# Attention projections as seven block products: four of the six projections of each layer in two pairs, pooling inputs and gates between them, pooled tiles and gates through DRAM

## The chip, the core and the metric

The kernel runs on one core of one Trainium2 chip. A core has five engines that run side by side, each taking its own instructions strictly in the order in which they were queued: TensorE (PE in the profile; PEld is its loading of weights), VectorE (DVE), ScalarE (ACT), GpSimd (POOL) and SyncE (SP), which here issues nearly all transfers between DRAM and the on-chip memories. The metric is the device time of one execution in microseconds, lower is better.

## The reference, cut to what matters

Two layers run over 512 tokens of 1024 channels. Each layer is a half-step feed-forward block, a mixer, and another half-step feed-forward block. The change is in the mixer:

```python
proj = h @ w_in                      # h: 512 x 1024
qa, ka, va, ub, qc, kc, vc, f_lin, g_lin = split(proj)   # six of 512 columns, ub 512, f 8, g 3 x 1024
ya = chunked_attention(qa, ka, va, rel_bias)     # 8 heads of 64
yb = pool_w(trailing_means(ub) - ub)             # 4 groups, windows 2, 4, 8, 16
yc = forgetting_attention(qc, kc, vc, f_lin)     # 8 heads of 64
merged = sum_n sigmoid(g_n) * (y_n @ w_branch_n) # n = a, b, c
x += gate2 * (merged @ w_out)
```

So the mixer multiplies the same `h` with weights for six attention projections, four pooling inputs of 128 channels, and 24 gate tiles of 128 channels. The result must agree with 32-bit floats.

## The kernel before, in words

Activations are kept transposed, as channels (partitions) by tokens. The kernel multiplies in a rounded 32-bit format: each operand is split into a rounded part `hi` and a remainder `lo`, and one 32-bit product is three matmuls, hi*hi, hi*lo and lo*hi (`triple`, L119 to L121). The normalised `h` lies split in `hhi` and `hlo`, as eight blocks of 128 channels. A weight chunk (`wchunk`, L266 to L279) is a transfer of 512 KB into a `raw` buffer (two of them), a cast on ACT to `whi` and a subtraction on DVE to `wlo` (three buffers each). A large pool of 17 buffers of 4 KB a partition, tag `b`, holds nearly everything else.

The code is Python that emits instructions in program order. A planner then orders each engine's queue by its own simulated times: an instruction that would wait can be overtaken by a later one whose operands are ready, and among ready ones the earlier in the program goes first. The programmer steers it by the order in the program, by `later(delay, fn)`, which emits `fn` when the counter `pe[0]` of issued matmuls (in units of one matmul of 512 columns) has advanced by `delay`, and by explicit orderings (`issue_after`). `behind(...)` in `wchunk` puts a chunk's cast and subtraction behind the newest piece of the norm.

The mixer (`Mixer.run`) goes in this order. (1) `norm.back` finishes `h` in two token halves, eight pieces each, with one ACT and two DVE instructions a piece (L371 to L374). (2) Three projections one after the other, `proj_qk` for qa and ka and `proj_v` for va, each four chunks of weights and 32 triples of 512 columns, with tokens as the stationary side; the first one starts on the first token half while the second is being normalised. The eight log-forget columns (`forget`) lie between them. Queries and keys get a norm per head (a square on ACT, a sum on DVE at L808, a Newton iteration of small DVE instructions at L293 to L295, a scaling at L826), and are then transposed on PE and split (`turn`, L831 to L846). (3) `attention` for branch a: 32 tiles of logits, and between them a generator of filler matmuls, nine units for each tile. Its filler is the projections qc, kc and vc. (4) `attention` for branch c; its filler is the gates and the merge of branch a. (5) After that the four pooling inputs (`pool_front`: 24 matmuls, then sums over shifted columns on POOL at L1033, then DVE), the gates and merge of c, and the gates and merge of b (`merge_units`; a gate is 24 matmuls and a tanh, a merge step 12 matmuls). (6) The output projection.

Beside this run the 144 modulation products, called dots here (`mod_step`, L206): each a 512 KB transfer and one DVE instruction over 1024 elements. `side_work` emits them in credit units as weight chunks are asked for: at rate `MOD_RATE` in the feed-forward blocks, and one a chunk in the merges of c and b. `mod_need` emits at once all that are still missing where they are needed.

The feed-forward blocks already use block products: two gate or up tiles and `h` are cut in two each way, and `seven` computes their product with seven block products in place of eight, from sums and differences of blocks of the weights (S1 to S4) and of `h` (T1 to T4, made by `Blocks` at L452 to L477 and kept split in eight `b` buffers).

## Time and profile before

| | us |
|---|---|
| median of 3 runs (lowest, highest) | 2408.19 (2405.26, 2410.62) |
| the profiled execution | 2409.17 |
| its span from the first to the last instruction | 2407.4 |
| PE busy (matmuls) | 2361.9 (98%) |
| PE loading weights | 2086.8 (87%) |
| DVE busy | 1728.9 (72%) |
| ACT busy | 1197.8 (50%) |
| POOL busy | 351.7 (15%) |
| HBM read, written | 312.16 MB, 6.38 MB |

The granted TensorE clock was 0.999 over the span. In this execution the first layer's mixer begins its projections at about 372 us and reaches the output projection at about 775 us; the second layer's is about 1190 us later. Matmuls are pipelined, so a matmul's recorded time is longer than the distance to the next one; the distance from start to start is what it costs when others follow. The table of stretches gives for each stretch its length, then for each engine the busy time and, in brackets, the number of instructions, then the granted clock, the busy share of the transfer engines and GB/s. The timeline gives start, duration, engine, line, operation, output and inputs, and in square brackets how long the engine had been idle before and what ended that. The list of waits gives total, count and longest.

### The profile page before, as it was taken

Reading aid. Unit: us, or ns where it says so; the run is one execution under the profiler, and the core shown is the slowest. Engines: PE = TensorE matmul, PEld = TensorE weight load, DVE = VectorE, ACT = ScalarE, POOL = GpSimd, SP = SyncE. Lnnn points to the kernel's source line nnn. Section 1 sums busy time; section 2 is a strip of 40 time slices with the busy share of each in tenths; the row PEclk is TensorE's granted clock in tenths of the full one; section 3 lists DMA queues with packets and bytes.
Section 4 is the critical chain, followed back from the end, with each engine's and each line's share of the span. In section 5 each row is a group of like instructions: output and inputs, shape, how many; then the busy total and the mean of one; then the engine's idle time right before and its main releaser. Section 6 shows DMA issues by size and latency. Waiting matters only on the chain. (4 is left out here: it accounts for less than half of the span.)

```text
span 2407.4 us, 36815 instructions
## 1 busy us (share of the span) xinstructions
PE 2361.9 (98%) x14106; PEld 2086.8 (87%) x14106; DVE 1728.9 (72%) x3070; ACT 1197.8 (50%) x2090; POOL 351.7 (15%) x423
## 2 busy tenths in 40 slices
PE   7999999999999999999999999999999999999999
PEld 5898988778878898989998989888788788989898
DVE  8987886787665476878577868777866755658583
ACT  5353545786632353535543636466765324536352
POOL 3000011144432210000100000112444322000000
PEclk9999999999999999999999999999999999999999
DMA  7534362323345524343325343623233554223322
GB/s 274 201 106 175 106 219 88 93 79 107 109 171 200 175 99 156 108 165 105 132 87 185 105 165 104 215 83 102 74 120 104 198 182 168 71 97 106 101 95 103
DMA packets 116436, 320.93 MB, mean 133 GB/s; under 512 B 11138, under 2 KB 13314, under 8 KB 116260
## 3 DMA queue, kind: packets, MB, share of 16 engines
q1 hardware_dynamic: 115106, 314.38, 38.8%
q0 software_dynamic: 1152, 4.19, 0.5%
q8 instruction: 111, 1.82, 0.3%
q14 instruction: 65, 0.53, 0.1%
q10 hardware_dynamic: 2, 0.00, 0.0%
HBM read 312.16 MB, written 6.38 MB: 132 GB/s over the span
## 5 line engine op out<-in xcount | busy, mean ns | idle before, releaser
L277 ACT CAST whi<-raw 128x1024 fp32r<-128x1024 f32 (+1 forms) x267 | 277.5, 1043 | 449.6 <-PE acc L120 251.7
L279 DVE TENSOR_TENSOR wlo<-raw,whi 128x1024 fp32r<-128x1024 f32 x259 | 321.1, 1242 | 168.2 <-ACT whi L277 165.0
L119 PE MATMUL acc<-b,whi 128*128 128x512 f32 (+1 forms) x960 | 361.8, 377 | 3.8 <-ACT whi L277 3.8
L121 PE MATMUL acc<-b,wlo 128*128 128x512 f32 (+1 forms) x960 | 358.0, 373 | 0.6 <-DVE wlo L279 0.6
L120 PE MATMUL acc<-b,whi 128*128 128x512 f32 (+1 forms) x960 | 358.5, 373 | 0.0
L119 PEld LDWEIGHTS acc<-b,whi 128*128 128x128 f32 x960 | 181.4, 189 | 36.0 <-ACT whi L277 4.6
L121 PEld LDWEIGHTS acc<-b,wlo 128*128 128x128 f32 x960 | 181.7, 189 | 33.1 <-DVE wlo L279 1.5
L120 PEld LDWEIGHTS acc<-b,whi 128*128 128x128 f32 x960 | 181.8, 189 | 30.1
L119 PE MATMUL acc<-hhi,whi 128*128 128x512 f32 x480 | 191.3, 400 | 7.2 <-DVE b L1051 3.1
L120 PE MATMUL acc<-hlo,whi 128*128 128x512 f32 x480 | 188.0, 392 | 1.1 <-DVE hlo L711 1.1
L121 PE MATMUL acc<-hhi,wlo 128*128 128x512 f32 x480 | 187.7, 392 | 0.3 <-DVE wlo L279 0.3
L385 DVE TENSOR_TENSOR ptb<-v,ptb 128x1024 fp32r<-128x1024 f32 x128 | 156.5, 1223 | 36.4 <-ACT ptb L384 36.2
L384 ACT CAST ptb<-v 128x1024 fp32r<-128x1024 f32 x128 | 134.1, 1050 | 92.8 <-DVE v L452 47.9
L384 ACT CAST whi<-raw 128x1024 fp32r<-128x1024 f32 (+1 forms) x128 | 106.7, 833 | 99.3 <-PE acc L120 56.2
L119 PE MATMUL acc<-whi,hhi 128*128 128x512 f32 x336 | 137.8, 411 | 0.9 <-DVE xv L385 0.9
L206 DVE CUSTOM_DVE_ANT_0 v<-v,b,badac 128x1024 f32<-128x1024 f32 x96 | 127.2, 1333 | 12.3 <-DMA v<-in_w_ada_dram 12.0
L121 PE MATMUL acc<-whi,hlo 128*128 128x512 f32 x336 | 131.9, 393 | 0.0
L120 PE MATMUL acc<-wlo,hhi 128*128 128x512 f32 x336 | 131.7, 392 | 0.0
L385 DVE TENSOR_TENSOR wlo<-raw,whi 128x1024 fp32r<-128x1024 f32 (+1 forms) x128 | 121.7, 950 | 6.4 <-ACT whi L384 4.6
L434 DVE SCALAR_TENSOR_TENSOR xv<-acc,modc,xv 128x512 f32<-128x512 f32 (+1 forms) x112 | 77.2, 690 | 64.1 <-PE acc L121 64.1
L119 PEld LDWEIGHTS acc<-hhi,whi 128*128 128x128 f32 x480 | 90.7, 189 | 26.1 <-DVE b L1051 4.0
L329 POOL TENSOR_TENSOR ssum<-ssum,t 128x256 f32<-128x256 f32 (+1 forms) x45 | 46.9, 1043 | 442.4 <-ACT t L328 442.2
(315 smaller groups left out, 6664.5 us busy)
## 6 DMA issues: line engine op xcount, KB each, us to landing
v<-in_w_ada_dram SPq DMA_DIRECT2D x96, 512.0 KB, 5.0
raw<-in_w_down_dram SPq DMA_DIRECT2D x88, 512.0 KB, 3.7
raw<-in_w_up_dram SPq DMA_DIRECT2D x82, 512.0 KB, 3.6
raw<-in_w_gate_dram SPq DMA_DIRECT2D x79, 512.0 KB, 3.6
raw<-in_w_ubg_dram SPq DMA_DIRECT2D x56, 512.0 KB, 3.5
b<-in_w_ada_dram SPq DMA_DIRECT2D x48, 512.0 KB, 4.7
raw<-in_w_qkv_dram SPq DMA_DIRECT2D x42, 512.0 KB, 3.8
raw<-in_w_branch_dram SPq DMA_DIRECT2D x24, 512.0 KB, 3.7
```

The source lines that it names most:

```text
L119: mm(o, lh, rh, start=start, stop=False)
L120: mm(o, lh, rl, start=False, stop=False)
L121: mm(o, ll, rh, start=False, stop=stop)
L206: dot = nc.vector.tensor_tensor_reduce(out=raw, in0=raw, in1=silc[0], scale=1.0, scalar=badac[:, l, j, d:d + 1], op0=ALU.mult, op1=ALU.add ...
L277: nc.scalar.copy(hi, raw)
L279: lo_eng.tensor_tensor(lo, raw, hi.bitcast(F32), op=ALU.subtract)
L329: nc.gpsimd.tensor_tensor(self.ssum[:, cols], self.ssum[:, cols], q, op=ALU.add)
L384: nc.scalar.copy(hi, src)
L385: nc.vector.tensor_tensor(lo, src, hi.bitcast(F32), op=ALU.subtract)
L434: nc.vector.scalar_tensor_tensor(x, acc_j, gate, x, op0=ALU.mult, op1=ALU.add)
```

## The change

The projections va and vc (columns 2 and 5 of the weights), and then qa and ka (columns 0 and 1), are computed as two pairs by a new function `wide`. Its `split_chunk` is the cast and subtraction of `wchunk`. A pair is a product of a 512 x 1024 `h` with 1024 x 1024 weights, cut in two each way. Seven block products P1 to P7 make it; each is 24 matmuls of 512 columns, so a pair is 168 in place of 192. The weights' sums and differences are made on DVE for each half product from unsplit chunks, and then split. The blocks T1 to T4 of `h` come from `Blocks`, now used in the mixer too; its steps are reordered so that T1 and T3 come first. Partial results are copied from PSUM to SBUF by ACT, the others added to them by DVE; `Values` and `Keys` then split the sums for attention. vc thus moves from the filler of attention a to the front. qc and kc stay there as before.

Between the block products stand other matmuls: all four pooling inputs behind P2 of the first pair, the first four gates of branch a (one after P6 of the first pair, one after P5 of the second, two at the end), and `forget`. The pooled tiles are made some 60 units later, with their shifted sums on DVE where they were on POOL, and go through DRAM until the merge. The gates of branch a are kept in DRAM too and read back as pairs; gates 4 to 7 of a fill attention a in vc's place, the gates of c fill attention c beside the merge of a, and the gates of b are made behind attention c. The dots of the merges start in the second half of attention c. In the feed-forward blocks the dots' rate in the down products goes from 1.0 to 1.9, 1.2, 1.6 and 1.2.

```diff
+    th_dram = [dr.tile([3, 4, P, 2 * T], F32, name=f"th_dram{l}") for l in range(L)]
+    u_dram = [dr.tile([4, P, 2, T], F32, name=f"u_dram{l}") for l in range(L)]
...
-            steps = ((self.h, 0), (self.h, 2), (self.t1_t3, 0), (self.split, 0), (self.t2_t4, 0), (self.split, 2))
-            self.todo = [lambda fn=fn, i=i + m: fn(i) for m in range(2) for fn, i in steps]
+            one = ((self.h, 0), (self.h, 2), (self.t1_t3, 0), (self.split, 0))
+            two = ((self.t2_t4, 0), (self.split, 2))
+            self.todo = [lambda fn=fn, i=i + m: fn(i) for steps in (one, two) for m in range(2) for fn, i in steps]
...
-                MOD_RATE[0] = 1.0
+                MOD_RATE[0] = (1.9, 1.2, 1.6, 1.2)[2 * l + s]
...
+    class Values:
...
+        def done(self, t):
+            b = st([P, H, 2, HD], F32R, self.tag, 4)
+            a3 = self.sums[:, t, :].rearrange("p (h d) -> p h d", h=H)
             for odd in range(2):
+                split_to(b[:, odd::2, odd, :], b[:, odd::2, 1 - odd, :], a3[:, odd::2, :])
...
+    class Keys:
...
+        def done(self, t, a=None):
+            a = self.sums[:, t, :] if a is None else a
             sq = t2(T)
             nc.scalar.activation(sq, a, AF.Square)
+            nc.vector.tensor_reduce(self.ss[:, t, :], sq.rearrange("p (h d) -> p h d", h=H), axis=AX.X, op=ALU.add)
...
+    def qkv_raw(l, col, kh, c, tag):
+        side_work()
+        raw = st([P, 2, T], F32, tag, {"b": NB, "raw": NRAW}[tag])
+        r0 = (4 * kh + 2 * c) * P
+        src = w_qkv[l, r0:r0 + 2 * P, col * T:(col + 1) * T].rearrange("(k p) c -> p k c", p=P)
+        last["dma"] = nc.sync.dma_start(raw, src).ins
+        return raw
+    def wide(l, cols, outs, blocks, order, pre=None):
+        first, second = outs
+        banks = {}
+        kept = {"a21": [], "s1": []}
+        two = (0, 1)
+        def bank(name):
+            if name not in banks:
+                banks[name] = [(mmt if name == "y" else acc)() for _ in two]
+            return banks[name]
+        def product(name, left, right, start):
+            o = bank(name)
+            for c in two:
+                hi, lo = left(c)
+                pairs = [(t, kk) for t in two for kk in two]
+                for n, (t, kk) in enumerate(pairs + pairs):
+                    bh, bl = blocks.operand(right)[2 * c + kk]
+                    tk = slice(t * P, (t + 1) * P)
+                    poll()
+                    if n < 4:
+                        mm(o[t], bh[:, tk], hi[:, kk, :], start=start and c == 0 and kk == 0, stop=False,
+                           skip_group_check=True)
+                        mm(o[t], bl[:, tk], hi[:, kk, :], start=False, stop=False, skip_group_check=True)
+                        pe[0] += 2.0
+                    else:
+                        mm(o[t], bh[:, tk], lo[:, kk, :], start=False, stop=c == 1 and kk == 1,
+                           skip_group_check=True)
+                        pe[0] += 1.0
+        def copy_out(name, out, t0, done=False):
+            for t in two:
+                nc.scalar.copy(out.sum_tile()[:, t0 + t, :], banks[name][t])
+                if done:
+                    out.done(t0 + t)
+        def add_out(name, out, t0):
+            for t in two:
+                s = out.sum_tile()[:, t0 + t, :]
+                nc.vector.tensor_tensor(s, banks[name][t], s, op=ALU.add)
+                out.done(t0 + t)
+        def p1():
+            if pre is None:
+                kept["a11"] = [qkv_raw(l, cols[0], 0, c, "b") for c in two]
+                product("x", lambda c: split_chunk(kept["a11"][c]), "B11", True)
+            else:
+                kept["a11"] = [p[2] for p in pre[:2]]
+                product("x", lambda c: pre[c][:2], "B11", True)
+            copy_out("x", first, 0)
+        def p2():
+            def left(c):
+                if pre is not None:
+                    return kept["a12"][c]
+                raw = qkv_raw(l, cols[0], 1, c, "raw")
+                parts = split_chunk(raw)
+                if "s2" in kept:
+                    minus(kept["s2"][c], raw, kept["s2"][c])
+                    kept["s4"] = kept["s2"]
+                return parts
+            product("y", left, "B21", True)
+            add_out("y", first, 0)
+        def left5(c):
+                if "ready" in kept and c == 0:
+                    return kept["ready"]
+                a21 = qkv_raw(l, cols[1], 0, c, "b")
+                a22 = qkv_raw(l, cols[1], 1, c, "raw")
+                s1 = st([P, 2, T], F32, "b", NB)
+                nc.vector.tensor_tensor(s1, a21, a22, op=ALU.add)
+                kept["a21"].append(a21)
+                kept["s1"].append(s1)
+                return split_chunk(s1)
+        def prep5():
+            kept["ready"] = left5(0)
+        def p5():
+            product("w", left5, "T1", True)
+            copy_out("w", second, 2)
+        def p6():
+            kept["s2"] = kept["s1"]
+            def left(c):
+                minus(kept["s2"][c], kept["s1"][c], kept["a11"][c])
+                return split_chunk(kept["s2"][c])
+            product("x", left, "T2", False)
+            copy_out("x", first, 2)
+        def p7():
+            def left(c):
+                minus(kept["a11"][c], kept["a11"][c], kept["a21"][c])
+                return split_chunk(kept["a11"][c])
+            product("x", left, "T3", False)
+            add_out("x", second, 2)
+        def p3():
+            def left(c):
+                if "s4" in kept:
+                    return split_chunk(kept["s4"][c])
+                raw = qkv_raw(l, cols[0], 1, c, "raw")
+                minus(kept["s2"][c], raw, kept["s2"][c])
+                return split_chunk(kept["s2"][c])
+            product("w", left, "B22", False)
+            add_out("w", first, 2)
+        def p4():
+            product("x", lambda c: split_chunk(qkv_raw(l, cols[1], 1, c, "raw")), "T4", False)
+            copy_out("x", second, 0, True)
+        steps = {"P1": p1, "P2": p2, "P3": p3, "P4": p4, "P5": p5, "P6": p6, "P7": p7}
+        if pre is not None:
+            kept["a12"] = [pre[2][:2], split_chunk(qkv_raw(l, cols[0], 1, 1, "raw"))]
+        for step in order:
+            if callable(step):
+                step(prep5)
+            else:
+                steps[step]()
+        first.begin()
+        second.begin()
...
+    def inputs(l, i, bank, w=None):
+        hi, lo = w or wchunk(w_ubg[l, i], (KD, P))
+        o = bank()
         for k in range(KD):
-            triple(pu, hi[:, k, :], lo[:, k, :], hhi[:, k, :], hlo[:, k, :], k == 0, k == KD - 1)
+            triple(o, hi[:, k, :], lo[:, k, :], hhi[:, k, :], hlo[:, k, :], k == 0, k == KD - 1)
+            yield
+        return o
+    def pool_in(l, g, bank, w=None):
+        pu = yield from inputs(l, g, bank, w)
         u = st([P, T + 16], F32, "b", NB)
         nc.gpsimd.memset(u[:, :16], 0.0)
         nc.scalar.copy(u[:, 16:], pu)
+        later(60 + 16 * g, lambda: pool_front(l, g, u))
+    def gate_in(l, n, d, bank, dest=None):
+        pg = yield from inputs(l, 4 + n * KD + d, bank)
+        th = t1(T) if dest is None else dest
+        nc.scalar.activation(th, pg, AF.Tanh, scale=0.5)
+        if dest is None:
+            nc.sync.dma_start(th_dram[l][n, d // 2, :, (d % 2) * T:(d % 2 + 1) * T], th)
+    def gate_pair(l, n, q, tag):
+        g = blk(tag, F32)
+        nc.sync.dma_start(g, th_dram[l][n, q].rearrange("p (a t) -> p a t", a=2))
+        return g
...
-            nc.gpsimd.tensor_tensor(nx[:, 16:], cur[:, 16:], cur[:, 16 - step:T + 16 - step], op=ALU.add)
+            nc.vector.tensor_tensor(nx[:, 16:], cur[:, 16:], cur[:, 16 - step:T + 16 - step], op=ALU.add)
...
-        b = st([P, 2, T], F32R, "ptb", 2)
+        b = blk("b")
         split_to(b[:, 0, :], b[:, 1, :], df)
-        return b
+        nc.sync.dma_start(u_dram[l][g], b.bitcast(F32))
...
-            self.pre = [qkv_chunk(self.l, 0, c, spare=t) for c, t in enumerate(("ptb", "ptb", "b"))]
+            self.pre = [qkv_chunk(self.l, 2, c, spare=t, keep=True) for c, t in enumerate(("ptb", "ptb", "b"))]
...
-            drain(proj_qk(l, 0, g8[:, 0:1], True, qa, self.pre, self.norm),
-                  proj_qk(l, 1, g[:, 1:2], False, ka), forget(l),
-                  proj_v(l, 2, "xv", va))
+            blocks = Blocks(self.norm.xa, modc[:, l, 3])
+            first_in = []
+            def ahead(_):
+                first_in.append(wchunk(w_ubg[l, 0], (KD, P)))
+            def second_half(prep):
+                self.norm.back(1, mmt)
+                blocks.schedule(4, 4)
+                drain(pool_in(l, 0, mmt, first_in[0]), pool_in(l, 1, mmt), pool_in(l, 2, mmt))
+                prep()
+                drain(pool_in(l, 3, mmt))
+                blocks.finish()
+            ga = [lambda _, d=d: drain(gate_in(l, 0, d, mmt)) for d in range(4)]
+            self.norm.back(0, mmt)
+            later(FRONT2, lambda: self.norm.front(1, mmt))
+            later(BACK2, lambda: self.norm.back(1, mmt))
+            wide(l, (2, 5), (Values("xv", va), Values("v2", vc)), blocks,
+                 (ahead, "P1", "P2", second_half, "P5", "P6", ga[0], "P3", "P7", lambda _: drain(forget(l)), "P4"), self.pre)
+            wide(l, (0, 1), (Keys(g8[:, 0:1], True, qa), Keys(g[:, 1:2], False, ka)), blocks,
+                 ("P1", "P5", ga[1], "P6", "P2", "P7", "P3", "P4"))
+            ga[2](None)
+            ga[3](None)
             finish_turns()
             turns.clear()
             heads[0] = 0
 
             def fill_a():
-                yield from proj_qk(l, 3, g8[:, 2:3], True, qc)
-                yield from proj_qk(l, 4, g[:, 3:4], False, kc)
-                yield from proj_v(l, 5, "v2", vc)
+                yield from proj_qk(l, 3, Keys(g8[:, 2:3], True, qc))
+                yield from proj_qk(l, 4, Keys(g[:, 3:4], False, kc))
+                for d in range(4, KD):
+                    yield from gate_in(l, 0, d, acc)
...
+            def gates_a(d):
+                yield
+                return m[d // 2][:, d % 2, :]
...
+            gb, gc = [], []
             def fill_c():
-                yield from merge_units(l, 0, ya, put_a)
-
-            attention(qc, kc, vc, lambda h: strip_c(l, h), yc, fill_c(), FILL_C, "c")
+                m.extend(gate_pair(l, 0, q, "xv") for q in range(4))
+                for d in range(3):
+                    yield from gate_in(l, 2, d, acc)
+                yield from merge_units(l, 0, ya, put_a, gates_a)
+                for d in range(3, KD):
+                    yield from gate_in(l, 2, d, acc)
+            pooled = []
+            def start_dots():
+                silc[0] = st([P, D], F32, "b", NB)
+                nc.sync.dma_start(silc[0], sil_dram.broadcast_to([P, D]))
+                in_ffn[0], mod_tag[0], MOD_RATE[0] = True, "b", 1.0
+            attention(qc, kc, vc, lambda h: strip_c(l, h), yc, fill_c(), FILL_C, "c",
+                      {4: start_dots})
             finish_turns()
             turns.clear()
+            wp = wpool_load(l)
+            for gi in range(4):
+                pooled.append(blk("b"))
+                nc.sync.dma_start(pooled[gi].bitcast(F32), u_dram[l][gi])
+            for d in range(4):
+                if d % 2 == 0:
+                    gb.append(blk("b", F32))
+                drain(gate_in(l, 1, d, acc, gb[d // 2][:, d % 2, :]))
             poll(True)
-            silc[0] = st([P, D], F32, "b", NB)
-            nc.sync.dma_start(silc[0], sil_dram.broadcast_to([P, D]))
-            wp = wpool_load(l)
-            mc = merge_units(l, 2, yc, put_c)
+            mc = merge_units(l, 2, yc, put_c, gates_c)
             for gi in range(4):
-                b = pool_front(l, gi)
-                later(60, lambda gi=gi, b=b: pool_back(l, gi, b, wp, yb))
-            in_ffn[0], mod_tag[0], MOD_RATE[0] = True, "b", 1.0
+                later(2 + 10 * gi, lambda gi=gi: pool_back(l, gi, pooled[gi], wp, yb))
             drain(mc)
             poll(True)
-            mb = merge_units(l, 1, yb, put_b)
+            mb = merge_units(l, 1, yb, put_b, gates_b)
             drain(mb)
```

248 lines of the change are left out of this document (119 added, 129 removed).

## The prediction

> **What bounds the kernel now.** First the page's busy times, then the stretches of the first layer's mixer, then single rows.
>
> ```profile
> PE   2361.9 (98%) x14106; PEld 2086.8 (87%) x14106; DVE 1728.9 (72%) x3070; ACT 1197.8 (50%) x2090; POOL 351.7 (15%) x423
> 160.00:170.00 10.00, 10.00 (x87) 10.00 (x86) 9.47 (x16) 6.33 (x11) 0.00 (x0) 1.00 0.34 105
> 300.00:345.00 45.00, 43.26 (x303) 40.06 (x302) 39.47 (x70) 19.88 (x32) 0.00 (x0) 0.98 0.61 207
> 372.00:394.00 22.00, 22.00 (x122) 18.65 (x121) 18.66 (x63) 11.62 (x27) 7.92 (x14) 1.00 0.13 50
> 394.00:447.00 53.00, 52.13 (x242) 41.39 (x242) 38.38 (x68) 35.14 (x50) 0.14 (x1) 1.00 0.31 96
> 447.00:545.00 98.00, 93.54 (x496) 76.49 (x495) 76.23 (x199) 74.85 (x164) 35.15 (x48) 1.00 0.29 87
> 545.00:640.00 95.00, 93.81 (x514) 79.16 (x513) 64.80 (x176) 60.36 (x150) 45.25 (x67) 1.00 0.35 115
> ```
>
> TensorE is busy for 98% of the span, and in the mixer's front (372 to 447 us: the three projections and forget) for 74.1 of 75 us. So matmuls are the time, and whoever removes one gains its place in the queue, if the other engines keep up. DVE is the one to watch: 57 of those 75 us, 76 of 98 in attention a, 65 of 95 in attention c. The first row is a feed-forward stretch with block products already in use: DVE 95% busy and PE not idle at all. A DVE that is nearly full does not by itself stop PE.
>
> What one matmul costs, from two rows of the second projection, 53 matmuls of 512 columns apart:
>
> ```profile
> 401.79 0.39 PE L119 MATMUL acc<-whi,hhi 128*128 128x512 f32 x1
> ...
> 413.80 0.39 PE L121 MATMUL acc<-whi,hlo 128*128 128x512 f32 x1
> ```
>
> 12.01 us by 53 is 0.227 us from start to start. That is my unit; 0.39 is only its length in the pipeline. The same holds on DVE:
>
> ```profile
> 159.44 0.68 DVE L385 TENSOR_TENSOR wlo<-raw,whi 128x512 fp32r<-128x512 f32 x1
> 160.04 0.68 DVE L452 TENSOR_TENSOR v<-raw,raw 128x512 f32<-128x512 f32 x1
> ...
> 163.65 0.42 DVE L515 TENSOR_TENSOR v<-v 128x256 f32<-128x256 f32 x1
> 163.99 0.42 DVE L515 TENSOR_TENSOR v<-mm,v 128x256 f32<-128x256 f32 x1
> ...
> 165.40 1.22 DVE L385 TENSOR_TENSOR ptb<-v,ptb 128x1024 fp32r<-128x1024 f32 x1
> 166.53 0.69 DVE L385 TENSOR_TENSOR b<-t,b 128x512 fp32r<-128x512 f32 x1
> ```
>
> Behind one another, a DVE instruction of 256, 512 or 1024 columns takes 0.34, 0.60 or 1.13 us from start to start, against 0.42, 0.68 and 1.22 recorded. Which of the two counts decides this case.
>
> **PE: what is removed.** A pair takes 7 x 24 = 168 matmuls in place of 192. Two pairs in two layers: 96 matmuls by 0.227 = 21.8 us less. All else on PE (pooling inputs, gates, merges, qc, kc) only changes place, matmul for matmul. Moved to the front, per layer: vc, four pooling inputs, four gates.
>
> **DVE: what is added.** Per layer 12 more weight splits (25 half products against 13 chunks of weights still to split in the front and vc), 16 sums and differences of weights, the blocks T (8 of 512, 4 of 1024), 12 additions of partial results, and 10 shifted sums from POOL: some 60 us, onto a DVE that had room for it over the layer, but mostly in the first pair. So I set DVE against PE there, from the end of P2 to the last split that P4 needs.
>
> PE: four pooling inputs, P5, P6, a gate, P3, P7, forget and half of P4, that is 244 units by 0.227 = 55.4 us, and 0.9 us that the row 394 to 447 shows idle already: 56.3.
>
> DVE, all of it earlier in the program than that last split:
>
> ```profile
> 386.87 1.08 DVE L371 TENSOR_TENSOR v<-mm,v 128x256 f32<-128x256 f32 x3 [0.79 <-PE mm L365]
> 387.89 0.50 PE L119 MATMUL acc<-ptb,hhi 128*128 128x512 f32 x1
> 393.60 2.36 DVE L279 TENSOR_TENSOR wlo<-raw,whi 128x1024 fp32r<-128x1024 f32 x2 [0.45 <-ACT whi L277]
> 441.15 1.21 DVE L902 TENSOR_TENSOR_SCAN t<-t 8x512 f32<-8x512 f32 x1
> ```
>
> - the rest of the second token half's norm: PE began that half at 387.89 us and DVE was through with it by about 393: 5 us
> - 1024 columns: splits of three pooling chunks, a gate, P4's two halves, T's four; in P5, P6, P3 and P7 two splits and two sums each: 26 by 1.13 = 29.4
> - 512 columns: T 8, additions after P2, P3 and P7 6, pooling 1+2+3+4 shifted sums and two more a tile: 32 by 0.60 = 19.2
> - 256 columns: two splits for each of six value tiles: 12 by 0.34 = 4.1
> - eight small pooling instructions, 1.2; forget's ten, of which the scan's 1.21 is the longest, 5 (estimate)
>
> Together 63.9 us against 56.3: PE waits 7.6 us a layer. From below: the pooled tiles (12 us of these 63.9) aren't needed until the merge; if they slipped into the second pair there would be no wait. From above: with recorded durations the list is 31.7 + 22.1 + 5.0 + 1.4 + 5.4 + 5.5 = 71.1, a wait of 14.8. I take 7.6, since the starts show the shorter steps, and the planner takes what is earlier in the program first.
>
> [...] The rows above, 0.60 us apart at 0.68 us recorded, speak for the shorter step.
>
> **The second pair.** DVE: 17 splits and 8 sums of 1024 (28.3), 6 additions, 8 sums of squares and 8 scalings of 512 (13.2), the last value tiles 1.4, 24 small Newton steps 4.8: 47.7 us against 240 units = 54.5 of PE. It keeps up. Its end is new: keys are complete only with P4, and before attention a lies nothing but two gates, 48 units = 10.9 us, where before it was all of va (96 units).
>
> ```profile
> 429.66 0.18 DVE L816 TENSOR_SCALAR nt_v<-qss 128x32 f32<-128x32 f32 x1
> ...
> 436.11 1.89 DVE L826 TENSOR_TENSOR ptb<-ptb,nt_z 128x512 f32<-128x512 f32 x3
> 448.40 1.40 ACT L840 ACTIVATE b<-mm,qkgc 64x512 fp32r<-64x512 f32 x2
> ```
>
> Behind P4: copies and squares on ACT some 2.4 us, a sum 0.6, small steps of both 4.8 (one alone took 429.66 to 436.11 with other work between), scalings 4.8, two gate splits 2.3: 14.9 us, 4.0 too much. Then all four turns of the queries stand ahead of the first key's: 16 ACT instructions by 0.70, 11 us, in which PE has only the filler qc, if its casts came first. So between nothing and 15 us; three chunks' buffers hold 16 us of filler, and the old transposes waited too. I take 2.5 a layer.
>
> **ACT, transfers, queues.** ACT had 46.8 of 75 us in the front; 16 more casts, the copies and the T blocks fill a longer stage to some 75%: nothing, as long as DVE is the later one. Added traffic is 3 MB of weights and 12 MB of gates and pooled tiles a layer, in stretches with a transfer share of 0.13 to 0.35: nothing. All go by SP's queue; a gate's write waits there for its tanh, and weight loads behind it with it. A load lands in 3.8 us, and a half product lasts 12 units = 2.7, with two `raw` buffers ahead; P6, P7 and most of P1 and P3 don't need them. If that cover were gone, each such write would cost up to 3 us.
>
> **What goes away.**
>
> ```profile
> PE acc L119 <- ACT whi L277: 6.2, 4, 2.3
> PE acc L119 <- DVE b L1051: 3.1, 2, 1.6
> 560.64 1.05 ACT L277 CAST whi<-raw 128x1024 fp32r<-128x1024 f32 x1
> 561.74 0.50 PE L119 MATMUL acc<-hhi,whi 128*128 128x512 f32 x1 [1.19 <-ACT whi L277]
> 689.77 2.05 DVE L206 CUSTOM_DVE_ANT_0 b<-b,b,badac 128x1024 f32<-128x1024 f32 x1
> ```
>
> PE's wait for pooled outputs, 3.1 us in both layers. The wait at 560 us behind vc's value splits, 1.4 in each layer with the matmul's ramp, 2.8. At 300 to 345 us the first feed-forward block emitted its ten missing dots at once (`mod_need` wants 32, the credits had given 22); at rate 1.9 they give 34, so the longest of those four waits, 2.3, goes. Added: in attention c some six dots a layer, 1.3 to 2.05 us each, on a DVE busy 65 of 95 us; I put 1 us a layer, from 0 to 6.
>
> **The sum.** -21.8 + 2 x 7.6 + 2 x 2.5 - 3.1 - 2.8 - 2.3 + 2 = -7.8 us. The profiled execution took 2409.2 (span 2407.4, and 1.8 around it), so 2401.4; the median of the runs is 1.0 lower: 2400.
>
> **Rivals.**
>
> *All hidden.* The pooled tiles slip, fillers cover the turns: -21.8 - 8.2 + 2 = -28, 2380 us. For it: the row at 160 us. Against it: they stand earlier in the program, and their inputs sit in `b` buffers that the weights wait for.
>
> [...]
>
> *Buffers.* At P5 T holds 8 `b` buffers, the weights' blocks 6, pooling inputs up to 4 and a pooled tile 1: 19 of 17.
>
> ```profile
> DMA to landing us min/median/max: 2.9/3.3/3.7
> ```
>
> A pooled tile's buffer returns when its write has landed, 3.3 us by the writes and reads of x. One such wait a layer that PE feels gives 2407, two 2413.
>
> **Chances and range.** Forecast 0.45, all hidden 0.15, DVE too slow 0.22, buffers 0.18. A difference under 0.2% (4.8 us) is about what a measurement can't tell from none. The forecast's own range is 2392 to 2408, of it 0.38 below 2403; with the hidden case 0.53 faster. The buffer case lies half within the bound, half slower: 0.17 same, 0.30 slower. The range runs from 2380 to 2420, to the rivals at either end.
>
> **What would show it.** 96 fewer matmuls of 512 columns. In the front, PE idle in the stretch behind P2 by some 8 us a layer, put down to DVE (wlo or hlo); DVE there over 95% busy. In the second pair PE full. A wait of 2 to 4 us at the first logits. No PE wait on L1051's successor, none near 340 us. I am wrong if PE waits on transfers into `b`, on ACT, or if attention a, with DVE's late turns in it, grows by over 3 us.

## The result, and the profile after

The change made the kernel slower: 2438.61 us (2436.46 to 2443.77 in four runs) against 2408.76 (2405.26 to 2410.62). The ratio is 1.0134, 95% interval 1.0122 to 1.0146. The prediction was 2400, with 2380 to 2420 as its range.

The busy times of the changed kernel's page, and then its table of stretches, with the columns as before: front, attention a, attention c, and from there into the output projection, first layer. (In the kernel before the output projection begins at about 819 us, behind the last merge step on DVE, and not at 775.)

```profile
PE 2361.7 (97%) x14010; PEld 2077.7 (85%) x14010; DVE 1836.0 (75%) x3194; ACT 1245.1 (51%) x2154; POOL 357.5 (15%) x403
```

```profile
374.30:533.50 159.20, 149.53 (x682) 120.57 (x682) 138.37 (x239) 99.99 (x154) 18.56 (x31) 0.99 0.40 131
533.50:636.40 102.90, 94.14 (x498) 75.11 (x497) 83.09 (x218) 79.01 (x181) 42.74 (x58) 0.98 0.27 88
636.40:735.90 99.50, 94.67 (x506) 78.36 (x505) 68.20 (x175) 56.84 (x140) 50.98 (x63) 1.00 0.57 183
735.90:852.20 116.30, 112.99 (x508) 92.77 (x508) 73.55 (x110) 38.37 (x57) 35.89 (x21) 1.00 0.63 220
```

The same four stretches of the kernel before:

```profile
372.00:454.20 82.20, 81.33 (x396) 66.06 (x395) 63.33 (x141) 52.03 (x87) 8.67 (x17) 1.00 0.28 88
454.20:559.80 105.60, 101.14 (x546) 83.12 (x546) 81.64 (x220) 80.15 (x182) 40.92 (x56) 1.00 0.28 83
559.80:655.10 95.30, 94.11 (x514) 79.32 (x512) 61.99 (x169) 58.89 (x147) 45.98 (x72) 1.00 0.35 117
655.10:835.30 180.20, 177.19 (x790) 145.99 (x789) 105.81 (x154) 59.47 (x84) 49.34 (x39) 1.00 0.51 177
```

Exactly 96 matmuls are gone, yet PE's busy time is the same to 0.2 us: matmuls of 512 columns behind a wait are recorded with some 0.50 us (410.02 below) and those at half clock with 0.63 (near 120 us, in the last section), where most have 0.39, so it doesn't show the loss. In the front PE is idle for 9.7 of 159.2 us (before 0.9 of 82.2), and attention a, with 48 matmuls fewer, is only 2.7 us shorter.

To compare stretches with different work I use their *excess*: length less 0.446 ns a column of their matmuls (0.228 us for 512, which is the mean from start to start in both traces where no wait comes between). It holds PE's waits, and also matmuls that are small (of 256 columns they start 0.120 us apart, 0.47 ns a column) or run at half clock (0.43 us apart). Worked out from the starts of all matmuls, first / second layer:

| stretch | before: length, excess | after: length, excess | excess, change |
|---|---|---|---|
| front | 82.2, 4.6 / 82.0, 4.6 | 159.3, 16.1 / 156.8, 13.9 | +11.5 / +9.3 |
| attention a | 105.5, 16.5 / 105.8, 16.8 | 102.9, 24.6 / 103.0, 24.6 | +8.1 / +7.8 |
| attention c | 95.3, 9.5 / 95.4, 9.6 | 99.5, 14.4 / 99.9, 14.8 | +4.9 / +5.2 |
| into the output projection | 180.2, 3.4 / 180.9, 4.1 | 116.3, 4.6 / 120.2, 8.5 | +1.2 / +4.4 |
| excess of all else, to the whole span | 74.8 | 74.6 | -0.2 |

Together +52.2 us of excess, less 21.9 us of matmuls: +30.3, the time by which the span grew. So the gain came in full and was given back almost two and a half times. Where PE waits longest, from the lists of waits, after and then before:

```profile
PE acc L121 <- DVE wlo L282: 8.9, 4, 3.5
PE mm L1138 <- ACT ptb L1120: 7.5, 6, 1.6
PE mm L121 <- DVE wlo L282: 5.0, 4, 1.8
...
PE acc L911 <- ACT whi L876: 4.4, 2, 2.5
...
PE mm L1138 <- DVE ptb L1121: 4.0, 2, 2.0
```

```profile
PE acc L119 <- ACT whi L277: 6.2, 4, 2.3
...
PE acc L119 <- DVE b L1051: 3.1, 2, 1.6
```

Three kinds are new: chunk splits and casts in the front (`mm` L121, L911), splits behind attention c (`acc` L121, 7.6 of its 8.9 us), and the attentions' own chain (L1138). The waits on pooled outputs (L1051) are gone.

### The profile page after: what moved, and what is told of

Its sections match the earlier page's. It is cut to its first block, busy times and chain, and to the rows that moved or that the text cites. A ratio compares the mean times of both kernels' runs of the same rounds, so it can differ in the third digit from the quotient of the medians.

```text
span 2437.7 us, 37073 instructions
## 1 busy us (share of the span) xinstructions
PE 2361.7 (97%) x14010; PEld 2077.7 (85%) x14010; DVE 1836.0 (75%) x3194; ACT 1245.1 (51%) x2154; POOL 357.5 (15%) x403
## 5 line engine op out<-in xcount | busy, mean ns | idle before, releaser
L280 ACT CAST whi<-raw 128x1024 fp32r<-128x1024 f32 (+1 forms) x241 | 249.5, 1039 | 390.1 <-PE acc L120 150.6
L282 DVE TENSOR_TENSOR wlo<-raw,whi 128x1024 fp32r<-128x1024 f32 x233 | 288.0, 1239 | 143.2 <-ACT whi L280 138.9
L121 PE MATMUL acc<-b,wlo 128*128 128x512 f32 (+1 forms) x960 | 356.9, 372 | 1.3 <-DVE wlo L282 1.3
L121 PEld LDWEIGHTS acc<-b,wlo 128*128 128x128 f32 x960 | 181.1, 189 | 33.6 <-DVE wlo L282 1.7
L121 PE MATMUL mm<-hhi,wlo 128*128 128x512 f32 x408 | 159.3, 391 | 5.0 <-DVE wlo L282 5.0
L119 PE MATMUL mm<-hhi,whi 128*128 128x512 f32 x408 | 160.0, 393 | 3.2 <-ACT whi L280 3.2
L120 PE MATMUL mm<-hlo,whi 128*128 128x512 f32 x408 | 159.1, 390 | 0.0
L387 ACT CAST whi<-raw 128x1024 fp32r<-128x1024 f32 (+1 forms) x128 | 106.5, 832 | 94.7 <-PE acc L120 53.4
L119 PE MATMUL acc<-hhi,whi 128*128 128x512 f32 x352 | 146.8, 419 | 1.7 <-ACT hhi L712 1.7
L121 PE MATMUL acc<-hhi,wlo 128*128 128x512 f32 x352 | 140.5, 399 | 7.7 <-DVE wlo L282 7.6
L209 DVE CUSTOM_DVE_ANT_0 v<-v,b,badac 128x1024 f32<-128x1024 f32 x100 | 132.3, 1331 | 13.6 <-DMA v<-in_w_ada_dram 13.5
L120 PE MATMUL acc<-hlo,whi 128*128 128x512 f32 x352 | 140.0, 398 | 0.7 <-DVE hlo L715 0.7
L1104 POOL TENSOR_SCALAR t<-t,rs 128x128 f32<-128x128 f32 (+2 forms) x96 | 100.3, 1045 | 204.9 <-DVE rs L1102 173.9
```

Source lines behind the costliest of these rows:

```text
L119: mm(o, lh, rh, start=start, stop=False)
L120: mm(o, lh, rl, start=False, stop=False)
L121: mm(o, ll, rh, start=False, stop=stop)
L209: dot = nc.vector.tensor_tensor_reduce(out=raw, in0=raw, in1=silc[0], scale=1.0, scalar=badac[:, l, j, d:d + 1], op0=ALU.mult, op1=ALU.add ...
L280: nc.scalar.copy(hi, raw)
L282: lo_eng.tensor_tensor(lo, raw, hi.bitcast(F32), op=ALU.subtract)
```

## The experiments

Kernels that ran once are compared by stretch rather than by their one time: the changed kernel's own four runs lie 7 us apart, and outside the mixers, where they are alike, these kernels differ by up to 7 us.

**The new order, without block products.** All four projections plain, in the changed order, with the matmuls of the kernel before.

```diff
-            wide(l, (2, 5), ..., self.pre)
-            wide(l, (0, 1), ...)
+            drain(proj(l, 2, Values("xv", va).evac, self.pre, self.norm),
+                  *[pool_in(l, i, mmt) for i in range(4)],
+                  proj(l, 5, Values("v2", vc).evac))
+            ga[0](None)
+            drain(forget(l), proj_qk(l, 0, Keys(g8[:, 0:1], True, qa)))
+            ga[1](None)
+            drain(proj_qk(l, 1, Keys(g[:, 1:2], False, ka)))
...
```

> The changed kernel with the four projections as plain products again, in the changed order (va, four pooling inputs, vc, a gate, forget, qa, a gate, ka, two gates): 48 matmuls more a layer (10.9 us of PE), some 53 us of recorded DVE work less. If the block products' DVE work is what costs: front and attention a no longer than the changed kernel's 262 although PE has 10.9 more, the kernel at 2420 to 2436. If the new order is what costs and the block products give what they remove: the kernel at 2455 to 2462.

2433.8 us. The front has no waits (excess 3.0 and 2.9), but attention a has an excess of 22.9 and 20.1, c 13.9 and 14.1, and the stretch behind it 7.6 and 7.2. Beside the kernel before (2405.6 beside it) the changed order with all that comes with it (gates through DRAM, earlier dots, new rates) costs 28 us, and block products in it 5 us more instead of 21.8 less. Front and attention a, 258.3 us against 262.2, and the time lie where the theory of the block products' cost had them. But the order is not free either: it costs 28 us, and the block products 26.6, to save 21.8.

**Each pair alone.** Only the first pair as blocks, then only the second (the other plain as above).

> The changed kernel with the second pair (queries and keys of attention a) as two plain projections of 96 matmuls each, one behind the other, and the first pair (the values) as block products: 24 matmuls a layer more than the changed kernel, 10.9 us in both. With all four plain in the same order the time was 2433.8, with both pairs as blocks 2438.6, though 21.8 us of matmuls were gone: some 15 us of waits a layer are theirs, of which the weights' sums are 4 to 5. Theory F, the other waits are those of the pooling stage behind P2, where casts, sums and T blocks stand behind the norm: they stay here, and the second pair's matmuls come on top: 2443 to 2449, front 157 to 162 us, its excess over pure matmul time about 13 to 16. Theory E, they come from the end of the front, where queries and keys become complete together and all eight turns are left: with plain queries first, half of the turns lie beside the keys' matmuls, and the waits go: 2421 to 2428, front and attention a together with an excess of 29 to 31 us in place of 40.7. Half each: 2432 to 2438.

> The mirror image: the values plain (the first on the first token half while the norm ends), the T blocks made beside the pooling inputs as before, and queries and keys as block products. Theory F: no waits in the pooling stage, so 2421 to 2428, front and attention a together with an excess of 29 to 31 us. Theory E: the turns still fall behind P4: 2441 to 2448, and an excess of 36 to 40 us, with matmuls missing before the first logits. Half each: 2432 to 2438.

2448.9 and 2434.8 us. Beside the plain order, the first pair raises the front's excess from 3.0 to 15.5 and from 2.9 to 13.2, attention a's hardly: 10 to 12 us a layer for 5.4 us of matmuls saved. The second raises front and attention a together by 3.3 and 4.6 us, about what it saves. With the second pair alone these two stretches have 29.2 and 27.6 us of excess, near the 29 to 31 of theory F, but the time fell into the range for half each: the matmuls saved were paid for there, and attention c and the stretch behind it have 3 us more, over both layers, than in the plain order. PE's waits in the front, first with only the first pair as blocks, then with only the second:

```profile
PE acc L911 <- ACT whi L876: 3.3, 1, 3.3
PE mm L121 <- DVE wlo L282: 2.5, 2, 1.8
PE mm L368 <- DVE strip L354: 1.7, 1, 1.7
PE acc L119 <- ACT ptb L922: 1.4, 1, 1.4
PE mm L119 <- ACT whi L280: 0.9, 1, 0.9
```

```profile
PE mm L858 <- DVE b L874: 1.0, 2, 0.6
```

Theory F holds for the front: its waits are the first pair's, most of them behind P2. In the changed kernel's timeline they look so (DVE, PE, SP's queue, ACT):

```profile
405.87 2.36 DVE L388 TENSOR_TENSOR b<-v,b 128x1024 fp32r<-128x1024 f32 x2
408.15 0.69 DVE L455 TENSOR_TENSOR v<-v 128x512 f32<-128x512 f32 x1
408.75 1.22 DVE L282 TENSOR_TENSOR wlo<-raw,whi 128x1024 fp32r<-128x1024 f32 x1
410.02 0.50 PE L121 MATMUL mm<-hhi,wlo 128*128 128x512 f32 x1 [1.83 <-DVE wlo L282]
410.03 0.33 SPq L269 DMA_DIRECT2D raw<-in_w_ubg_dram  x1
410.41 2.50 SPq L886 DMA_DIRECT2D b<-in_w_qkv_dram  x2
415.43 1.23 DVE L961 TENSOR_TENSOR b<-b,raw 128x1024 f32<-128x1024 f32 x1 [1.43 <-DMA b<-in_w_qkv_dram]
416.69 1.04 ACT L876 CAST whi<-b 128x1024 fp32r<-128x1024 f32 x1 [0.76 <-DVE b L961]
417.79 0.50 PE L911 MATMUL acc<-whi,b 128*128 128x512 f32 x1 [2.48 <-ACT whi L876]
```

A pooling chunk's split stands on DVE behind sums and splits of T. PE waits 1.83 us for it, and so does the `raw` buffer that it reads: SP's queue can issue the next load only at 410.03, and the weights of P5 stand behind that load. They land at 415.4, DVE has to wait 1.43 us for them, and PE 2.48. One late split became two waits.

**Mending that place.** (1) T's twelve steps spread wider; (2) two gates taken from between block products and put among the pooling inputs.

```diff
-                blocks.schedule(4, 4)
+                blocks.schedule(4, 8)
```

> The changed kernel with the twelve steps that make the blocks T of h spread over all four pooling inputs (one per 8 units of matmuls in place of one per 4). Theory T (in the pooling stage a chunk's subtraction stands on DVE behind sums and splits of T; it holds the `raw` buffer, SP's queue stands at the next load for it, and the weights of P5 behind that load come late): the waits of 1.99 and 2.64 us near 408 and 415 us shrink, front 2 to 4 us shorter in each layer: 2430 to 2435. Theory V (the steps between norm and P5 are simply too many for DVE, in whatever order): the waits move to P5 itself, 2437 to 2442.

```diff
-                drain(pool_in(l, 0, mmt, first_in[0]), pool_in(l, 1, mmt), pool_in(l, 2, mmt))
+                drain(pool_in(l, 0, mmt, first_in[0]))
+                ga[0](None)
+                drain(pool_in(l, 1, mmt))
+                ga[1](None)
+                drain(pool_in(l, 2, mmt))
...
```

> The changed kernel with the two gates that stand between block products (behind P6 of the first pair and behind P5 of the second) moved between the pooling inputs: 10.9 us more matmuls before P5, with 2.3 us more of DVE splits. Theory V (too many DVE and ACT steps between the second half of the norm and P5 for the matmuls there): the waits of 1.99 and 2.64 us at the last pooling inputs and P5 shrink and the front is 3 to 5 us a layer shorter, 2429 to 2434, unless P6 and P3, which lose their cover, wait in turn: then 2437 to 2442. Theory B (the waits come from single late steps, whatever the matmuls between): 2437 to 2440, the waits as long as before.

2448.3 and 2442.9 us. PE's waits in the front, first (1), then (2):

```profile
PE acc L911 <- ACT whi L876: 5.6, 2, 4.0
```

```profile
PE acc L911 <- ACT whi L876: 4.3, 4, 2.0
```

In (1) the wait of 1.83 us for the split is gone and P5's first wait is 1.6 us, but P5 waits 4.0 for its second weights, as theory V had it. In (2) both waits of about 2 us are gone and four others, the longest of 2.0, come at 463 to 479 us, where the gates had been cover. The front's excess did not fall: 15.6 and 16.0, then 16.5 and 17.9, against 16.1 and 13.9. Why the first also lengthened attention c of the second layer (18.5 of excess) is open.

**Less work for DVE.** The shifted sums of the pooled tiles back on GpSimd; then 16 sums and differences of weights left out.

```diff
-            nc.vector.tensor_tensor(nx[:, 16:], cur[:, 16:], cur[:, 16 - step:T + 16 - step], op=ALU.add)
+            nc.gpsimd.tensor_tensor(nx[:, 16:], cur[:, 16:], cur[:, 16 - step:T + 16 - step], op=ALU.add)
```

> The changed kernel with the ten shifted sums of the pooled tiles on POOL again, as before the change (7 us of DVE a layer less). Theory 3 (from the norm to the end of attention a, DVE is the bound: 246 us of recorded DVE work in 262 a layer): that stretch falls by 4 to 7 us a layer, the kernel by 8 to 14 against the changed kernel's 2438. Theory 4 (DVE is busy there but not the bound; chains through ACT and the planner's order are): within 4 us of 2438. By the earlier runs theory 1 in its strict form is out: with the first turns first attention a began 11 us earlier and lasted 12 longer.

```diff
-                s1 = st([P, 2, T], F32, "b", NB)
-                nc.vector.tensor_tensor(s1, a21, a22, op=ALU.add)
+                s1 = a21
...
-                minus(kept["s2"][c], kept["s1"][c], kept["a11"][c])
...
-                minus(kept["a11"][c], kept["a11"][c], kept["a21"][c])
...
-                minus(kept["s2"][c], raw, kept["s2"][c])
```

> The changed kernel with the 16 sums and differences of weights a layer left out (unsummed weights are split and multiplied, so the output is not the reference's); PE work, loads, casts and splits stay. 19.5 us of recorded DVE work a layer less. Theory 3: front and attention a together fall from 262 to 243 to 250 us a layer, the kernel to 2400 to 2415. Theory 4: they fall by less than 8 a layer, the kernel stays above 2422.

2443.1 and 2434.2 us. The first gained nothing. The second took 18 us of DVE's busy time from front and attention a of each layer, and the front became 3.6 and 2.2 us shorter, attention a 1.9, in the range of theory 4. So DVE's total isn't the bound, and no single place is: of these four edits three moved the wait to another product, and the fourth left most of it. What holds the front back is then a chain (load, sum, cast, split, with two `raw` buffers between) with little slack. That last sentence is argued from these four runs; no run took that chain apart.

**Attention a: its turns, its gates, its filler.** First, only the first turn ahead of the logits.

```diff
-            finish_turns()
+            finish_turns(0)
...
-            attention(qa, ..., FILL_A, "a")
+            attention(qa, ..., FILL_A, "a", {1: more})    # more: the remaining turns
```

> The changed kernel, where before attention a only the first of four turns of queries and keys is made, and the other three after the logits of head 0. Theory 1: the first logits of a come 6 to 10 us earlier in each layer and the length of a stays, so the kernel falls by 10 to 20, to 2418 to 2428. Theory 2 (filler already covers the turns on PE): within 4 us of 2438.

2442.1 us. The front is 11.8 us shorter and attention a 12.3 longer: front and a take 262.7 us against 262.2. The turns pushed behind the first logits change nothing.

```diff
-                 ("P1", "P5", ga[1], "P6", "P2", "P7", "P3", "P4"))
+                 ("P1", "P5", "P6", "P2", "P7", "P3", "P4"))
+            ga[1](None)
```

> The changed kernel with one gate (24 matmuls, 5.45 us of PE) moved from between P5 and P6 of the second pair to behind P4, so that three gates and not two lie between the last key product and attention a: the same matmuls, 16.3 us of cover and not 10.9 for the chain of norm and turns. Theory E: front and attention a together 3 to 5 us a layer shorter, 2429 to 2433. Theory F: nothing is gained, and P6's sums of weights lose the cover that the gate gave them: 2437 to 2444.

2437.8 us. One more gate behind P4: front and attention a 259.7 and 258.7 against 262.2 and 259.8 us. So the gate's place is worth 2.5 us at most, less than theory E had, and hardly more than these two stretches differ between kernels in which they are alike (262.8 and 261.2 with the dots moved, below).

```diff
-                for d in range(4, KD):
-                    yield from gate_in(l, 0, d, acc)
+                yield from phantom(4 * KD)    # counts as many units, emits nothing
```

> The changed kernel with the four gates left out that fill attention a (gates 4 to 7 of branch a; the first four are written in their places, so the output is not the reference's), the planner's counter advanced as if they were there: 96 matmuls of 512 columns a layer less, 21.8 us of PE, in attention a alone. Theory 1 (attention a has a length of its own, set by the chains of its 32 tiles on DVE and ACT, and filler in it costs little): from the first logits of a to the first of c it stays at 95 us or more against 102.9, the whole kernel at 2422 or more against 2438. Theory 2 (attention a is as long as its PE work plus waits that stay): it falls to some 81 us and the kernel to some 2395.

2405.6 us. Of the 21.9 us of matmuls that a layer lost, 8.2 were missing in attention a, since other filler moved up, and 13.7 in c; they became 9.0 and 7.8 us shorter. The result lies between the two theories: filler costs its own length in the one and more than half of it in the other, and is no free cover.

```diff
 # the kernel before: vc computed in the front, not in attention a
-                  proj_v(l, 2, "xv", va))
+                  proj_v(l, 2, "xv", va), proj_v(l, 5, "v2", vc))
...
-                yield from proj_v(l, 5, "v2", vc)
+                yield from phantom(4 * KD)
```

> The kernel before, with only the projection vc moved from the filler of attention a to the front, as a plain projection of 96 matmuls a layer; the counter is advanced in its place in the filler. The PE work is the same. Theory 1: the front grows by 22 us a layer and attention a shrinks by less than 8 of its 105.5, so 2408 becomes 2436 to 2452. Theory 2: what the front gains attention a loses, 2404 to 2414.

2422.9 us, 19.8 more than the kernel before beside it (2403.1), with the same matmuls. The front is 22.3 us longer, attention a and c 4.7 and 8.4 us shorter. Attention a shrinks as little as theory 1 had it; that c shrinks too, neither had. What is taken out of the attentions' filler isn't given back in full (13.1 of 22.3 us); I read this as the attentions then waiting on themselves.

Head by head, attention a's excess shows where its 8 us are (first layer, heads 0 to 7):

```
before  0.9 1.1 1.0 4.2 3.0 1.9 2.8 1.5
after   2.7 2.0 1.4 4.7 3.0 1.8 2.8 6.2
```

Heads 0 to 2 lack 47 of their 108 filler matmuls, which the planner had pulled ahead while PE waited for the turns. The largest piece is head 7. One theory fell on it before another held:

```diff
+                w = wchunk(w_ubg[l, 8], (KD, P))
                 for d in range(4, KD):
-                    yield from gate_in(l, 0, d, acc)
+                    ahead_w = wchunk(w_ubg[l, 5 + d], (KD, P)) if d + 1 < KD else None
+                    yield from gate_in(l, 0, d, acc, None, w)
+                    w = ahead_w
...
```

> The changed kernel with the weights of gates 4 to 7 of attention a's filler asked for one gate ahead. Theory G (the filler that took vc's place fetches, casts and splits each 512 KB chunk just in time, where vc held the weights of its last 48 matmuls ready): the last head of attention a, 18.6 us with 6.2 us over its pure matmul time against 13.9 and 1.5 in the kernel before, loses 3 to 4.5 us in both layers: 2430 to 2433. Theory L (that head is long because its last turns and the chain from logits to weights of attention end there, whatever the filler is): less than 1 us a layer, 2437 to 2441.

2440.9 us, head 7 with 6.0 and 6.4 us of excess: the weights' time of arrival is not it. In the trace of the changed kernel, DVE and GpSimd in that head:

```profile
624.90 0.42 DVE L1096 CUSTOM_DVE_ANT_0 t<-mm,strip 128x256 f32<-128x256 f32 x1 [2.58 <-POOL b L1145]
```

```profile
622.88 1.29 POOL L1078 TENSOR_TENSOR strip<-strip,cmask 128x128 f32<-128x128 f32 x3 [0.20 <-DMA strip<-fv_dram]
624.13 0.73 POOL L1145 TENSOR_TENSOR b<-t,b 64x256 fp32r<-64x256 f32 x1
```

DVE's step on the logits waits 2.58 us for a GpSimd instruction that it has no operand from: L1145 reads an output tile, and what DVE waits for is that tile's buffer. GpSimd comes to it late, behind the masks of attention c's strips. Logits, outputs and now the gates' tanh all take turns in the two `t1` buffers, and a gate's stays taken until its write to DRAM has landed (2.0 to 3.8 us from issue here). In attention c, whose gates do the same, DVE's wait is put down to such a write itself:

```profile
719.79 0.42 DVE L1096 CUSTOM_DVE_ANT_0 t<-mm,strip 128x256 f32<-128x256 f32 x1 [0.71 <-DMA th_dram<-t]
```

So the gates of attention a got a tile of their own:

```diff
-        th = t1(T) if dest is None else dest
+        own = n == 0 and d >= 4
+        th = dest if dest is not None else st([P, T], F32, "ssum", 1) if own else t1(T)
```

> The changed kernel with the results of gates 4 to 7 of attention a written to the tile `ssum`, idle there, in place of the two rotating `t1` buffers that the attention's logits and outputs use too. Theory R (a gate's tanh holds one of the two `t1` buffers until its write to DRAM has landed; the logits' next tile waits for the other, which GpSimd frees late: DVE stood 2.6 us for it in the last head of attention a): the last head falls from 18.6 to 14 to 16 us in both layers, 2429 to 2434. Theory L (the chain of the attention ends there whatever the gates write): less than 1 us a layer, 2437 to 2441.

2434.0 us. The stretch of attention a with that edit:

```profile
531.90:630.20 98.30, 92.00 (x499) 73.92 (x498) 82.01 (x217) 78.78 (x180) 43.25 (x58) 1.00 0.29 92
```

98.3 us in both layers against 102.9 and 103.0, and head 7 has 1.6 us of excess, as before the change. Theory R is shown, for 4.6 us a layer in this stretch. Not all of it arrives at the end: in this run front, attention c and the stretch behind it are 5.8 us longer together, over both layers, than in the changed kernel.

**The dots.** Started behind attention c and not in its fifth head.

```diff
-            attention(qc, ..., "c", {4: start_dots})
+            attention(qc, ..., "c")
             finish_turns()
             turns.clear()
+            start_dots()
```

> The changed kernel with its modulation dots starting behind attention c, as in the kernel before, and not in its fifth head. If the dots (DVE time, their loads, and DVE waiting for a load) make attention c longer, it goes from 99.5 us back to some 95.5 a layer and the kernel to some 2430. If it is the new filler (gates on their own, their tanh and writes), attention c stays at 99 or more and the kernel within 4 us of 2438.

2430.3 us. PE's waits in attention c, first the changed kernel, then this one:

```profile
PE mm L1138 <- ACT ptb L1120: 3.9, 3, 1.6
```

```profile
PE mm L1138 <- ACT ptb L1120: 0.7, 1, 0.7
```

Attention c takes 96.0 and 95.8 us, an excess of 10.2 and 10.0 against 14.4 and 14.8. So the dots cost 4.2 to 4.8 us a layer there.

With the shifted sums on GpSimd (the edit above) as well:

> The changed kernel with both the shifted sums on POOL and the dots behind attention c. If the two effects are apart (one in the front, one in attention c), their gains add up: 9 from the dots and what the sums alone give, 2417 to 2429 together.

2435.8 us: attention c is at 95.2. The two mixers take 950.3 us together, 950.1 with the dots alone; the 5 us more lie outside them, where both kernels are alike. So the sums on GpSimd neither gained nor cost anything that this run could show.

**The rates of the dots alone**, in the kernel before.

```diff
-                MOD_RATE[0] = 1.0
+                MOD_RATE[0] = (1.9, 1.2, 1.6, 1.2)[2 * l + s]
```

> The kernel before with nothing but the new rates of the dots in the down products (1.9, 1.2, 1.6 and 1.2 in place of 1.0). The bursts of missing dots near 340 and 1527 us, with waits of 2.1 and 3.3 us and the slow matmuls behind them, go; near 115 us stands a new wait of 3.0 us, as in the changed kernel. By the stages of the changed kernel: start to the first mixer 2.4 us longer, from the first output projection to the second mixer 1.4 us shorter, the end 0.5 shorter: 2403 to 2411 beside 2405 to 2409 before, that is no difference over 0.2%. Were the rates a gain, as the prediction had it with 2.3 us: 2402 to 2405.

2405.0 us (11 runs) against 2407.3 (15 runs): ratio 0.9991, interval 0.9982 to 1.0. That is 2.2 us, the size that the prediction gave the vanished bursts, but an interval that reaches to no difference. The burst near 340 us is gone; a new wait of 1.57 us ends at 119 us.

**Mends together.** First the blocks T spread, the gates' weights ahead and the dots behind attention c; then the gates' own tile, the gates among the pooling inputs and the dots.

> The two edits before and the dots behind attention c, in one kernel. The dots alone gave 8.3 us. If the causes are as theories G and T have them and add up: 2412 to 2420, still not under the kernel before. If attention a and the pooling stage keep their waits: 2428 to 2434.

> The two edits before and the dots behind attention c (which alone gave 8.3 us) in one kernel. By theories R and V together: 2412 to 2421. By R alone: 2420 to 2426. By neither: 2428 to 2434. None of them expects it under the kernel before (2403 to 2411).

2433.5 us (ratio 1.0113, interval 1.0096 to 1.013) and 2429.2 us (1.0097, 1.008 to 1.0114). The second has attention a at 98.3 and c at 95.1 and 96.2 us, as its parts gave alone, and a front as long as ever (159.9 and 157.9): there the excess is still 12.1 and 10.4 us above the kernel before, behind attention c 3.8 and 4.4. The second lies in the range given for neither theory, though attention a kept its gain: in its profile the mixers take 6.6 us less than with the dots alone, and all else 2.7 more. No version of the changed kernel here beats the kernel before.

## Why the prediction was wrong, step by step

*Matmuls, -21.8 us.* Right: 96 fewer, 21.9 us.

*First pair, a wait of 7.6 us a layer, at most 14.8.* The place was right (PE waits behind P2 for DVE's late steps), the account was not, and the term was too small: 12.5 and 10.3 us more excess in the front with that pair as blocks. I had balanced DVE against PE over the whole stretch from P2 to P4, so that PE waits for the surplus of a sum. Without the weights' sums this balance is 9.0 us lighter, 54.9 against 56.3, and leaves no wait; that kernel's front kept 12.5 and 11.7 us of excess, with shorter waits at the same places. The waits fell into the first 30 us, where the norm's second half, T, three splits and the sums for P5 meet:

```profile
396.00:425.00 29.00, 23.15 (x91) 17.68 (x90) 27.50 (x42) 16.87 (x25) 0.38 (x4) 0.94 0.39 127
425.00:520.00 95.00, 94.05 (x422) 76.34 (x421) 82.86 (x127) 56.31 (x81) 14.42 (x17) 1.00 0.46 146
520.00:533.50 13.50, 12.36 (x60) 9.28 (x59) 8.57 (x12) 13.16 (x21) 0.00 (x0) 1.00 0.26 93
```

DVE is busy for 27.5 of 29 us. 89 matmuls start there, 20.3 us by 0.228, so 8.7 us are lost: PE stands for 5.9, and behind the last wait the clock is at half for 3.4 us (hence 0.94), which costs 1.7. Another wait, of 1.7 us, lies just before, at the norm (L368), and one of 0.9 at 470 us. All these waits add up to 8.4 us. That this is near 7.6 is luck, since the balance that gave 7.6 does not carry them; and what a wait costs beyond its length stood in the sum at nothing. Behind 425 us DVE had room, as the rival *all hidden* said, but the pooled tiles' slip could no longer help. A mean over 56 us hid a peak of 29.

*Second pair full, 2.5 us a layer at its end.* Right to 1 or 2 us: the middle row shows PE full, and the pair costs 3.3 and 4.6 us in front and attention a. In the last row, with the turns, ACT is busy for 13.2 of 13.5 us. The wait of 2 to 4 us at the first logits did not come: the longest waits there are 0.35 us and, 7 us later, 0.99.

*Transfers and queues: nothing; attention a as before.* This is the step that failed in kind. I priced the gates' writes by SP's queue and found cover for it. Their price was the tile that they are written from: one of two `t1` buffers, 4.6 us a layer. And I took gates 4 to 7 as filler equal to vc, and held that all else on PE only changes place: vc as a plain projection ahead of attention a costs 19.8 us in all. The queue had a price too, at P5: DVE waits 1.43 us there for a load into `b` that was issued late, and PE through ACT 2.48. That is a sign of being wrong that the text itself named, PE waiting on transfers into `b` and on ACT. Its other alarm, attention a over 3 us longer, should read: its excess over 3 us greater. It is 8.

*Dots, 1 us a layer, 0 to 6.* Inside the bounds, mis-sized: 4.2 to 4.8.

*What goes away, -8.2 us.* The waits on pooled outputs and the burst near 340 us did go. But something was late next each time: behind attention c, DVE now waits for a dot's load and the splits stand behind it,

```profile
817.14 1.28 DVE L209 CUSTOM_DVE_ANT_0 b<-b,b,badac 128x1024 f32<-128x1024 f32 x1 [2.11 <-DMA b<-in_w_ada_dram]
...
818.58 1.23 DVE L282 TENSOR_TENSOR wlo<-raw,whi 128x1024 fp32r<-128x1024 f32 x1
```

```profile
819.86 0.50 PE L121 MATMUL acc<-hhi,wlo 128*128 128x512 f32 x1 [3.20 <-DVE wlo L282]
```

The stretch has 1.2 and 4.4 us more excess, not 3 less in all; in the second layer 6.8 us at half clock come with such a wait of 3.54. With the dots behind attention c waits of 3.2 and 3.1 us remain there. The rates' 2.3 us is about what they gave alone, though it can't be told from none; in the changed kernel the stretches outside the mixers are only 0.2 us shorter in all.

*The sum.* Measured: -21.9 + 20.8 (front) + 15.9 (attention a) + 10.1 (c) + 5.6 (behind it) - 0.2 = +30.3. By the same stretches the forecast was -21.8 + 20.2 (front and attention a) - 0.8 - 3.1 - 2.3 = -7.8: front and a are 16.5 us worse, c 10.9, the stretch behind it 8.7. Of attention a's 15.9, shared buffers are 9.3; the rest lies in heads 0 to 3, whose filler was pulled ahead. Of c's 10.1, the dots are 9.0. *DVE too slow*, with its 0.22 the case behind the upper end of the range, took every DVE instruction at its recorded length: a wait of 14.8 us in the first pair and 4 for the turns, 2418 us by my estimate. It had the sign, but no run shows that price: by the starts DVE kept my shorter steps (408.15 to 408.75 is 0.60 us at 0.69 recorded). *Buffers* had the right kind of cause and the wrong pool: it counted `b`, not `t1`. What part of the front's 20.8 us comes from which link of its chain stays open, and so does most of the 5.6 us behind attention c.

## What to carry to other kernels

Balance the engines over the stretch in which the new work must be done, not over the stage: 29 us at 95% of DVE cost PE nearly 9, though the stage had room for all of it. When a result is newly sent to DRAM, price the buffer that it sits in until the write has landed (2.0 to 3.8 us from issue here, worth 4.6 us a layer in attention a), and count who else takes turns in that pool; the release showed in this trace as an engine waiting for an instruction whose result it does not read (DVE 2.58 us for L1145). Filler in a stage that waits on its own chain wasn't free cover here (21.9 us of it less a layer made the two attentions 16.8 us shorter): compare stretches by length less matmul time, head by head, before moving work in or out.

## What the hardware showed

Behind some of its waits PE ran at half speed for some microseconds. In the changed kernel, near 115 us:

```profile
114.61 0.39 PE L120 MATMUL acc<-b,whi 128*128 128x512 f32 x1
116.32 0.50 PE L121 MATMUL acc<-b,wlo 128*128 128x512 f32 x1 [1.32 <-DVE wlo L282]
...
118.86 0.79 PE L119 MATMUL acc<-b,whi 128*128 128x512 f32 x1 [1.34 <-ACT whi L280]
119.45 0.63 PE L120 MATMUL acc<-b,whi 128*128 128x512 f32 x1
119.88 0.63 PE L119 MATMUL acc<-b,whi 128*128 128x512 f32 x1
120.30 0.63 PE L120 MATMUL acc<-b,whi 128*128 128x512 f32 x1
```

```profile
119.00:122.00 3.00, 3.00 (x7) 2.33 (x8) 3.00 (x6) 1.05 (x1) 0.00 (x0) 0.50 0.05 22
```

The starts are 0.43 us apart, not 0.227, and the granted clock of the stretch is 0.50. So behind these waits more was lost than their length. It was not always so: behind the wait of 3.20 us at 819.86 the next matmuls start 0.23 us apart, and the clock did not change (the stretch from 735.9 to 852.2 has a granted clock of 1.00).

In the kernel before the clock is at half in two stretches of 3.4 us, behind waits of 1.44 and 2.33 us, and after the change in four of 3.4 and one of 6.8 us (granted 0.999 and 0.996 over the span). At half speed that is 3.4 and 10.2 us lost: 6.8 of the 52.2 us of excess. What decides which wait brings it, these runs don't show.
